# Sums of a Strassen key and value product: formed on VectorE in place of GpSimd

## The chip, the core and the metric

The kernel runs on one core of a Trainium2 chip. The metric is the device time of one execution in microseconds (us), lower is better. Before the change three runs gave 1868.92, 1868.02 and 1868.57 us, a median of 1868.57.

## What is computed

The reference is a decoder trunk of two layers on a stream `x` of 512 tokens by 2048 channels, in float32. The first layer is sparse attention, the second stick-breaking attention. Between them one set of keys and values is computed from the stream, and the change lies in this product:

```python
def shared_kv(x, w_kv):
    b, s, _ = x.shape
    k, v = jnp.split(x @ w_kv, [KVW_B], axis=-1)      # 512x2048 @ 2048x1024
    return k.reshape(b, s, N_KV_B, HEAD_DIM), v.reshape(b, s, N_KV_B, HEAD_DIM)

def mixer_b(x, w_in, w_o, k, v):
    q, gate = jnp.split(x @ w_in, [WIDTH_B], axis=-1)
    ...
```

The queries of `mixer_b`, `x @ w_in[:, :2048]`, are computed right around it: their first 512 columns before, the other three chunks of 512 columns after.

## The kernel before, in words

**Matmuls in parts.** Every float32 operand is split into a high and a low part (`split`, line 140): ScalarE copies the source to the high part, VectorE subtracts that from the source to give the low part. `mm3` (line 144) then makes three matmuls, at lines 145, 146 and 147. Weights stream in from HBM by DMAs from SyncE's queue (`next_raw`, line 191), one 128x2x512 tile for each. The parts of weights are in tiles `wh`/`wl` and `sh`/`sl` of three buffers each, so that ScalarE can write the next part only when TensorE has read an old one.

**The key and value product** is one Strassen step (Winograd's form) of seven half-size products m1 to m7 in place of eight. The stream is cut into halves of tokens and of channels, the weights into halves of rows and into the key and the value columns. `kv_items` (line 423) makes the weight operands in the order in which TensorE takes them: first plain blocks for m2 and m4, then blocks and one difference for m1 and m7, and last, for each of eight k, the three sums of `sums` (line 454). It takes two tiles of weights, r0 and r1. s1 is formed by GpSimd (line 458), s2 and s4 by VectorE (lines 459 and 460); s2 reads s1, and s4 reads s2. Each of the three is then split and used in six matmuls, 18 for each k, for m6, m5 and m3 (`gemm_quarters`, line 471). `sums` for the next k is called ahead of the third split of this one. Every second tile of these weights has its home in the `f` tiles, which is why DMAs and operations of this pass name `f`.

**The last additions.** Keys are gathered in c11 and c12, values in c21 and c22 (they lie in the tiles `E`), each 128x1024. ScalarE copies products out of PSUM into them; VectorE adds m1 to c11, m6 to u (which holds m1), and m5 to c22, in pieces of 128x512. GpSimd makes five 128x1024 additions between tiles of SBUF: c21 + c22 (line 1314) when m7 is out, and behind the last product c21 + u, c22 + u, c12 + t3 and c12 + u (lines 1332 to 1335; t3 holds m3).

**The next Strassen chunks.** The three other query chunks follow at once. In each, a unit is one raw tile: VectorE forms two sums from the raw tile (`prepare`, lines 396 and 397, tile `st`), then s2 and s4 (lines 404 and 405), and these and the plain blocks are split into two items of weights. An item is seven terms of three matmuls with 256 columns, 21 in all: the first two terms use `wh`/`wl`, the next four `sh`/`sl`, the last `wh`/`wl` again. A chunk has 8 units, so 16 items. The two items of unit 0 are made while the key and value pass still has a few matmuls to go (line 1320). The first two sums of unit 1 are not prepared ahead (`u % 8 != 1`, line 417): they come behind the m6 and m5 additions in VectorE's line.

**Order.** Instructions of each engine run in the order of its queue. TensorE's order is written out by hand. On the other engines a scheduler may move instructions, but what runs while `pinned` is set, as through `paced` (line 355), keeps its place. `bg` is a queue of pieces of work: `pumped_at` (line 368) wraps a run of matmul steps (one step is one `mm3`) and issues one piece at each of the listed steps; for the Strassen chunks these are steps 13, 20, 27, 34, 41, 53 and seven later ones of 112 (line 1346). `drain` issues what is left at a chunk's end. In the first chunk `bg` is empty. The keys are read next in the second chunk (`turn_keys`, line 1337) and the values in the third (`split_values`).

Of the kernel before, what the change touches and what calls it, by code (L numbers as in the profile page):

```python
# [14 lines left out]
ALU = mybir.AluOpType  # L15
# [62 lines left out]
def trunk_kernel(  # L78
# [48 lines left out]
    act, dve, pool = (Paced(e) for e in (nc.scalar, nc.vector, nc.gpsimd))  # L127
    pool = nc.gpsimd
# [11 lines left out]
    def split(hi, lo, src, eng=dve):  # L140
        act.activation(hi, src, AF.Copy)
        eng.tensor_tensor(lo, src, hi.bitcast(F32), ALU.subtract)
# [48 lines left out]
    def next_raw():  # L191
        while sent[0] < len(units) and len(raws) < (6 if sent[0] in kv_units else 3):
            raw = homes.get(sent[0])
            if raw is None:
                raw = top.tile([128, 2, 512], F32, name="raw", tag="raw", bufs=3)
            unit = units[sent[0]]
            if len(unit) == 1:
                _, k, n = unit[0].shape
            else:
                k, n = 2, unit[-1]  # L200
            raw = raw.rearrange("p a n -> p (a n)")[:, : k * n].rearrange("p (k n) -> p k n", k=k)
            if len(unit) == 1:
                nc.sync.dma_start(raw, unit[0])
            else:
                src, a, b, c0, n = unit
                rows = src.rearrange("(k p) n -> p k n", p=128)
                step = b - a
                if sent[0] < 2:

                    for i, cut in enumerate(((0, H if sent[0] else NSEL, T), (0, T))):  # L210
                        for lo, hi in zip(cut, cut[1:]):
                            halves.append((raw[:, i, lo:hi], rows[:, a + i * step, c0 + lo : c0 + hi]))
                    if len(halves) == 6:
                        for n in (1, 3, 4, 2, 5, 0):
                            nc.sync.dma_start(*halves[n])
                else:
                    nc.sync.dma_start(raw, rows[:, a : b + 1 : step, c0 : c0 + n])
            raws.append(raw)
            sent[0] += 1
        return raws.popleft()  # L220
# [38 lines left out]
    def weight_parts():  # L259
        return tuple(top.tile([128, 512], F32R, name=n, tag=n, bufs=3) for n in ("wh", "wl"))  # L260
# [92 lines left out]
    bg = deque()  # L353

    def paced(fn, *args):
        was, pinned[0] = pinned[0], True
        fn(*args)
        pinned[0] = was
# [64 lines left out]
    def kv_items(wp):  # L423

        made = [0]
        temps = [F[1][:, n] for n in range(4)]
        for _ in range(2):
            st = wp.tile([128, 4 * H], F32, name="st", tag="st", bufs=2)
            temps.extend(st[:, n * T : (n + 1) * T] for n in range(2))

        def temp():
            made[0] += 1
            return temps[made[0] % 8]

        def parts(n, src):
            if n % 2:
                pair = weight_parts()
            else:
                pair = [wp.tile([128, 4, 128], F32R, name=n, tag=n, bufs=3).rearrange("p a n -> p (a n)") for n in ("sh", "sl")]
            split(*pair, src)  # L440
            return pair

        for k in range(8):
            raw = next_raw()
            for a in range(2):
                yield parts(a, raw[:, a])
        for k in range(8):
            raw = next_raw()
            s3 = temp()
            dve.tensor_tensor(s3, raw[:, 0], raw[:, 1], ALU.subtract)  # L450
            yield parts(0, raw[:, 0])
            yield parts(1, s3)

        def sums():
            r0 = next_raw()
            r1 = next_raw()
            s1, s2, s4 = temp(), temp(), temp()
            pool.tensor_tensor(s1, r0[:, 1], r1[:, 1], ALU.add)
            dve.tensor_tensor(s2, s1, r0[:, 0], ALU.subtract)
            dve.tensor_tensor(s4, r1[:, 0], s2, ALU.subtract)  # L460
            return s2, s1, s4

        ready = sums()
        for k in range(8):
            three = ready
            for n, src in enumerate(three):
                if n == 2 and k < 7:
                    ready = sums()
                yield parts(3 * k + n, src)
# [809 lines left out]
    with tc.tile_pool(name="sp", bufs=1) as sp:  # L1279
        Kf, Vf = shared  # L1280
        banks = [bank(b, "q") for b in range(4)]
        gemm = gemm_w(kitems, plain, banks, order=PAIRS)
        items = first_chunk(gemm, TF, T1, C3, lambda: Ahead(kv_items(sp), 4))
        for h in range(4):
            act.activation(F[0][:, h], banks[h], AF.Copy)


        def pair(first, name):
            return [bank(first + j, name) for j in range(2)]

        def half(row, t):
            return lambda k: (XH[k + row][:, t : t + H], XL[k + row][:, t : t + H])

        def summed(i):
            return lambda k: (C3[k][0][:, i], C3[k][1][:, i])

        c11, c12, c21, c22 = Kf[:, 0:2], Kf[:, 2:4], Vf[:, 0:2], Vf[:, 2:4]
        u, t3 = F[3][:, 2:4], F[1][:, 0:2]

        m2, m4 = pair(4, "m2"), pair(6, "m4")  # L1300
        run(gemm_quarters(items, ((half(8, 0), m2), (summed(2), m4))))
        for j in range(2):
            paced(act.activation, c11[:, j], m2[j], AF.Copy)
        for j in range(2):
            paced(lambda: act.activation(c21[:, j], m4[j], AF.Copy, scale=-1.0))

        m1, m7 = pair(0, "m1"), pair(2, "m7")
        run(gemm_quarters(items, ((half(0, 0), m1), (summed(1), m7))))
        for j in range(2):
            paced(act.activation, u[:, j], m1[j], AF.Copy)  # L1310
            paced(dve.tensor_tensor, c11[:, j], c11[:, j], m1[j], ALU.add)
        for j in range(2):
            paced(act.activation, c22[:, j], m7[j], AF.Copy)
        pool.tensor_tensor(c21, c21, c22, ALU.add)

        m6, m5, m3 = pair(4, "m6"), pair(6, "m5"), pair(0, "m3")
        gemm = gemm_quarters(items, ((summed(0), m6), (half(0, H), m5), (half(8, H), m3)))
        steps(gemm, 42)
        pinned[0] = True
        items = strassen_stream([512] * 3, sp).prime()  # L1320
        pinned[0] = False
        steps(gemm, 2)
        for j in range(2):
            paced(dve.tensor_tensor, u[:, j], u[:, j], m6[j], ALU.add)
        steps(gemm, 2)
        for j in range(2):
            paced(act.activation, c12[:, j], m5[j], AF.Copy)
            paced(dve.tensor_tensor, c22[:, j], c22[:, j], m5[j], ALU.add)
        run(gemm)
        for j in range(2):  # L1330
            paced(act.activation, t3[:, j], m3[j], AF.Copy)
        pool.tensor_tensor(c21, c21, u, ALU.add)
        pool.tensor_tensor(c22, c22, u, ALU.add)
        pool.tensor_tensor(c12, c12, t3, ALU.add)
        pool.tensor_tensor(c12, c12, u, ALU.add)

        def turn_keys(g):
            s = slice(g * 128, (g + 1) * 128)
            ps = bank(0, "kt")
            for t in range(4):  # L1340
                pe.transpose(ps[:, t * 128 : (t + 1) * 128], Kf[:, t, s], ident)
            act.activation(Kf[:, :, s], ps.rearrange("p (t s) -> p t s", t=4), AF.Copy)

        for n, dst in enumerate(F[1:]):
            M = product_banks(2 - n)
            gemm = pumped_at(gemm_s(items, C3, M), (13, 20, 27, 34, 41, 53, 65, 77, 89, 101, 104, 107, 110))
            if n == 1:
                steps(gemm, 40)
                for g in range(4):
                    steps(gemm, 16)  # L1350
                    turn_keys(g)
            run(gemm)
            drain()
            if n == 2:
                items = Ahead(gate_items(), 2).prime()
                combined = combine_last(sp, M, lambda i: quarter(dst, i))
            else:
                bg.extend(combine(sp, M, lambda i: quarter(dst, i)))
            if n == 1:

                bg.extend(lambda t=t: split_values(t) for t in range(4))
                bg.append(lambda: split_keys(0))
                bg.extend(lambda i=i: split_scaled(0, i) for i in (3, 1, 2))
# [298 lines left out]
```

## Time and profile before

| what | value |
|---|---|
| median of three runs | 1868.57 us (1868.02 to 1868.92) |
| the profiled execution, its time | 1868.31 us |
| its span, first to last instruction | 1866.6 us |
| mean granted TensorE clock | 0.998 |
| ScalarE busy | 940.0 us, 50% of the span |
| mean DMA rate | 106 GB/s |
| GpSimd, eight 128x512 additions at line 458 | 6.3 + 5.9 us |
| GpSimd, five 128x1024 additions | 2.4 to 2.8 us each |

How to read the rows below. PE is TensorE's matmuls, PEld its weight loads, DVE VectorE, ACT ScalarE, POOL GpSimd, SP SyncE. A timeline row gives the start in us from the span's beginning, the duration, the engine, the source line, the operation, output and inputs, and in brackets the idle time just before it with what ended it. `x2` on a timeline row is two merged instructions with their time together. A row of waits gives who waited for whom, the total in us, the number of waits, the longest. A row of groups gives busy us and the mean ns of one. A row of windows gives the stretch and its length, the busy time and count of PE, PEld, DVE, ACT and POOL, then the granted TensorE clock, the busy share of DMA and GB/s. Most operations pass through a helper that records them, so their line is L118 or L116; they are told apart by tiles.

### The profile page before, as it was taken

Reading aid. Unit: us, or ns where it says so; the run is one execution under the profiler, and the core shown is the slowest. Engines: PE = TensorE matmul, PEld = TensorE weight load, DVE = VectorE, ACT = ScalarE, POOL = GpSimd, SP = SyncE. Lnnn points to the kernel's source line nnn. Section 1 sums busy time; section 2 is a strip of 40 time slices with the busy share of each in tenths; the row PEclk is TensorE's granted clock in tenths of the full one; section 3 lists DMA queues with packets and bytes.
Section 4 is the critical chain, followed back from the end, with each engine's and each line's share of the span. In section 5 each row is a group of like instructions: output and inputs, shape, how many; then the busy total and the mean of one; then the engine's idle time right before and its main releaser. Section 6 shows DMA issues by size and latency. Waiting matters only on the chain.

```text
span 1866.6 us, 24141 instructions
## 1 busy us (share of the span) xinstructions
PE 1852.5 (99%) x8845; PEld 1561.0 (84%) x8845; DVE 1233.7 (66%) x2337; ACT 940.0 (50%) x1686; POOL 36.7 (2%) x41
## 2 busy tenths in 40 slices
PE   9999999999999999999999989999999999999998
PEld 8898888888888888888888879997888888888887
DVE  5668678566556444675467698888878745567534
ACT  3546333355554432475245534467888743347422
POOL 0000000000000000000000040001000000000000
PEclk9999999999999999999999999999999999999999
DMA  6441323222221432323335633322122252232323
GB/s 198 128 123 59 102 90 102 90 68 68 68 69 57 159 123 79 125 95 109 124 118 164 212 127 103 102 91 91 57 68 80 68 186 96 76 128 99 116 102 113
DMA packets 111431, 197.55 MB, mean 106 GB/s; under 512 B 8784, under 2 KB 29264, under 8 KB 111312
## 3 DMA queue, kind: packets, MB, share of 16 engines
q1 hardware_dynamic: 111312, 196.01, 32.7%
q8 instruction: 69, 1.13, 0.2%
q14 instruction: 50, 0.41, 0.1%
HBM read 187.60 MB, written 8.39 MB: 105 GB/s over the span
## 4 chain that ended last, share of the span: by engine, by line
PE 96%; DVE 2%; issue 1%; ACT 1%; DMA 0%; SPq 0%; DVEq 0%; ACTq 0%
PE g L145 12%; PE g L147 12%; PE g L146 12%; PE o L146 7%; PE o L145 7%; PE o L147 7%; PE q L147 4%; PE q L146 4%; PE q L145 4%; PE m L147 3%; PE m L146 3%; PE m L145 3%; PE iq L147 1%; PE iq L146 1%; PE iq L145 1%; PE pt L949 1%
## 5 line engine op out<-in xcount | busy, mean ns | idle before, releaser
L118 ACT ACTIVATE wh<-raw 128x512 fp32r<-128x512 f32 (+2 forms) x596 | 345.3, 580 | 660.7 <-PE g L146 219.6
L118 DVE TENSOR_TENSOR wl<-raw,wh 128x512 fp32r<-128x512 f32 (+2 forms) x595 | 372.9, 628 | 432.3 <-ACT wh L118 417.3
L145 PE MATMUL g<-xh,wh 128*128 128x512 f32 x1024 | 403.5, 394 | 0.0
L147 PE MATMUL g<-xh,wl 128*128 128x512 f32 x1024 | 399.5, 390 | 0.0
L146 PE MATMUL g<-xl,wh 128*128 128x512 f32 x1024 | 399.3, 390 | 0.0
L147 PEld LDWEIGHTS g<-xh,wl 128*128 128x128 f32 x1024 | 192.2, 188 | 40.9
L146 PEld LDWEIGHTS g<-xl,wh 128*128 128x128 f32 x1024 | 192.5, 188 | 37.4
L145 PEld LDWEIGHTS g<-xh,wh 128*128 128x128 f32 x1024 | 192.4, 188 | 36.9
L147 PE MATMUL o<-xh,wl 128*128 128x512 f32 x512 | 199.2, 389 | 0.0
L146 PE MATMUL o<-xl,wh 128*128 128x512 f32 x512 | 199.2, 389 | 0.0
L145 PE MATMUL o<-xh,wh 128*128 128x512 f32 x512 | 199.2, 389 | 0.0
L145 PE MATMUL q<-xh,wh 128*128 128x512 f32 x320 | 124.5, 389 | 0.0
L146 PE MATMUL q<-xl,wh 128*128 128x512 f32 x320 | 124.5, 389 | 0.0
L147 PE MATMUL q<-xh,wl 128*128 128x512 f32 x320 | 124.5, 389 | 0.0
L145 PEld LDWEIGHTS o<-xh,wh 128*128 128x128 f32 x512 | 96.1, 188 | 20.0
L147 PEld LDWEIGHTS o<-xh,wl 128*128 128x128 f32 x512 | 96.1, 188 | 20.0
L146 PEld LDWEIGHTS o<-xl,wh 128*128 128x128 f32 x512 | 96.1, 188 | 19.9
L146 PEld LDWEIGHTS q<-xl,wh 128*128 128x128 f32 x320 | 60.1, 188 | 12.6
L145 PEld LDWEIGHTS q<-xh,wh 128*128 128x128 f32 x320 | 60.1, 188 | 12.6
L147 PEld LDWEIGHTS q<-xh,wl 128*128 128x128 f32 x320 | 60.1, 188 | 12.3
L116 ACT ACTIVATE wk<-z 128x512 f32<-128x512 f32 x80 | 47.9, 598 | 38.7 <-DVE z L116 15.2
L118 DVE TENSOR_TENSOR xl<-f,xh 128x512 fp32r<-128x512 f32 x80 | 54.3, 686 | 12.6 <-ACT f L118 12.3
(341 smaller groups left out, 3237.1 us busy)
## 6 DMA issues: line engine op xcount, KB each, us to landing
raw<-w_in_a SPq DMA_DIRECT2D x95, 512.0 KB, 3.6
raw<-w_in_b SPq DMA_DIRECT2D x64, 512.0 KB, 3.7
raw<-w_ple_gate SPq DMA_DIRECT2D x52, 512.0 KB, 3.4
raw<-w_o_a SPq DMA_DIRECT2D x24, 512.0 KB, 3.4
raw<-w_o_b SPq DMA_DIRECT2D x24, 512.0 KB, 3.5
f<-w_kv_b SPq DMA_DIRECT2D x16, 512.0 KB, 4.1
raw<-w_kv_b SPq DMA_DIRECT2D x16, 512.0 KB, 3.8
raw<-w_ple_gate SPq DMA_DIRECT2D x24, 256.0 KB, 2.8
```

The source lines that it names most:

```text
L116: ins = method(*args, **kw)
L118: ins = method(*args, **kw)
L145: pe.matmul(out, a[0], b[0], start=start, stop=False)
L146: pe.matmul(out, a[0], b[1], start=False, stop=False)
L147: pe.matmul(out, a[1], b[0], start=False, stop=stop)
L949: pe.transpose(pt[:, h * 128 : (h + 1) * 128], P[i][:, h, kb * 128 : (kb + 1) * 128], ident)
```

## The change

Three edits. `sums` forms s1 on VectorE. The addition c21 + c22 at line 1314 and the two c22 + m5 additions at line 1328 are taken out. In place of the four GpSimd additions behind the last product, six VectorE additions of 128x1024 are appended to `bg`: c21 + c22 (c22 still holds m7 alone), c22 + c12 (c12 still holds m5), c12 + t3, c12 + u, c21 + u, c22 + u. So one is issued at each of the first six listed steps of the first Strassen chunk.

```diff
@@ -455,7 +455,7 @@
             r0 = next_raw()
             r1 = next_raw()
             s1, s2, s4 = temp(), temp(), temp()
-            pool.tensor_tensor(s1, r0[:, 1], r1[:, 1], ALU.add)
+            dve.tensor_tensor(s1, r0[:, 1], r1[:, 1], ALU.add)
             dve.tensor_tensor(s2, s1, r0[:, 0], ALU.subtract)
             dve.tensor_tensor(s4, r1[:, 0], s2, ALU.subtract)
             return s2, s1, s4
@@ -1311,7 +1311,6 @@
             paced(dve.tensor_tensor, c11[:, j], c11[:, j], m1[j], ALU.add)
         for j in range(2):
             paced(act.activation, c22[:, j], m7[j], AF.Copy)
-        pool.tensor_tensor(c21, c21, c22, ALU.add)
 
         m6, m5, m3 = pair(4, "m6"), pair(6, "m5"), pair(0, "m3")
         gemm = gemm_quarters(items, ((summed(0), m6), (half(0, H), m5), (half(8, H), m3)))
@@ -1325,14 +1324,11 @@
         steps(gemm, 2)
         for j in range(2):
             paced(act.activation, c12[:, j], m5[j], AF.Copy)
-            paced(dve.tensor_tensor, c22[:, j], c22[:, j], m5[j], ALU.add)
         run(gemm)
         for j in range(2):
             paced(act.activation, t3[:, j], m3[j], AF.Copy)
-        pool.tensor_tensor(c21, c21, u, ALU.add)
-        pool.tensor_tensor(c22, c22, u, ALU.add)
-        pool.tensor_tensor(c12, c12, t3, ALU.add)
-        pool.tensor_tensor(c12, c12, u, ALU.add)
+        for out, more in ((c21, c22), (c22, c12), (c12, t3), (c12, u), (c21, u), (c22, u)):
+            bg.append(lambda out=out, more=more: dve.tensor_tensor(out, out, more, ALU.add))
 
         def turn_keys(g):
             s = slice(g * 128, (g + 1) * 128)
```

## The prediction

> **What bounds the kernel now.** I began with the page, parts 1 and 4, and then asked for TensorE's own waits.
>
> ```profile
> PE 1852.5 (99%) x8845; PEld 1561.0 (84%) x8845; DVE 1233.7 (66%) x2337; ACT 940.0 (50%) x1686; POOL 36.7 (2%) x41
> PE 96%; DVE 2%; issue 1%; ACT 1%; DMA 0%; SPq 0%; DVEq 0%; ACTq 0%
> ```
>
> ```profile
> PE m L147 <- DVE wl L118: 5.9, 1, 5.9
> PE m L146 <- DVE wl L118: 1.1, 1, 1.1
> PE z L145 <- DVE t L116: 0.2, 1, 0.2
> ```
>
> TensorE is busy 99% of the span. VectorE or GpSimd can shorten the run only where TensorE stands still or runs slowly. From these waits, two such places matter, both for a low part `wl` from VectorE. The timeline of TensorE dates them (start, duration, instruction), and the windows give the granted clock (the third column from the right).
>
> ```profile
> 1078.87 0.39 PE L145 MATMUL m<-sh,xh 128*128 128x512 f32 x1
> 1080.23 0.39 PE L145 MATMUL m<-wh,xh 128*128 128x512 f32 x1
> 1081.72 0.50 PE L146 MATMUL m<-wl,xh 128*128 128x512 f32 x1 [1.10 <-DVE wl L118]
> ...
> 1107.62 0.28 PE L145 MATMUL m<-xh,wh 128*128 128x256 f32 x1
> 1112.83 0.28 PE L146 MATMUL m<-xl,wh 128*128 128x256 f32 x1
> 1118.98 0.58 PE L147 MATMUL m<-xh,wl 128*128 128x256 f32 x1 [5.88 <-DVE wl L118]
> 1124.84 0.28 PE L147 MATMUL m<-c,sl 128*128 128x256 f32 x1
> 1126.39 0.28 PE L145 MATMUL m<-xh,wh 128*128 128x256 f32 x1
> 1156.63 0.28 PE L145 MATMUL m<-xh,wh 128*128 128x256 f32 x1
> ```
>
> ```profile
> 1081.00:1083.00 2.00, 1.28 (x6) 1.06 (x7) 2.00 (x4) 0.00 (x0) 0.12 (x1) 1.00 0.68 258
> 1119.00:1121.00 2.00, 2.00 (x9) 2.00 (x10) 1.84 (x4) 1.47 (x4) 0.00 (x0) 0.50 0.00 0
> ```
>
> Place one is in the last key and value pass. Six matmuls take 1080.23 - 1078.87 = 1.36 us there, 0.227 each; the step from 1080.23 to 1081.72 is 1.49, so 1.26 are lost.
>
> Place two is the first Strassen chunk, which runs from 1107.62 (X below) to 1156.63, where the next begins: 49.01 us. It is 16 items of 21 matmuls. Twelve undisturbed items take 1156.63 - 1126.39 = 30.24, so 2.52 an item and 0.12 a matmul; 16 items would take 40.32. Lost: 8.69. Of this the wait is 6.03 (from 1112.83 + 0.12 to 1118.98). Another 2.6 is a clock of 0.50 after it: the 27 matmuls from 1118.98 to 1124.84 take 5.86 where 27 x 0.12 = 3.24 is normal.
>
> [...]
>
> Why was `wl` late? VectorE and GpSimd side by side:
>
> ```profile
> 1109.24 4.26 DVE L118 TENSOR_TENSOR st<-raw 128x256 f32<-128x256 f32 x2
> 1113.42 2.56 DVE L118 TENSOR_TENSOR st<-st,raw 128x256 f32<-128x256 f32 x1
> 1116.01 2.44 DVE L118 TENSOR_TENSOR st<-raw,st 128x256 f32<-128x256 f32 x1
> 1118.38 0.55 DVE L118 TENSOR_TENSOR wl<-raw,wh 128x384 fp32r<-128x384 f32 x1
> ...
> 1110.64 2.58 POOL L1334 TENSOR_TENSOR E<-E,f 128x1024 f32<-128x1024 f32 x1
> 1115.66 2.52 POOL L1335 TENSOR_TENSOR E<-E,f 128x1024 f32<-128x1024 f32 x1
> ...
> 1075.39 1.78 DVE L118 TENSOR_TENSOR f<-st,raw 128x512 f32<-128x512 f32 x1
> 1077.20 2.77 DVE L118 TENSOR_TENSOR f<-f,f 128x512 f32<-128x512 f32 x1
> 1079.90 1.76 DVE L118 TENSOR_TENSOR wl<-st,wh 128x512 fp32r<-128x512 f32 x1
> ...
> 1076.58 2.85 POOL L1314 TENSOR_TENSOR E<-E 128x1024 f32<-128x1024 f32 x1
> ```
>
> A VectorE addition that meets a GpSimd addition grows to the latter's length: 2.44 beside 2.52, 2.77 beside 2.85. The next groups show what these shapes take alone (mean ns last before the idle time).
>
> ```profile
> L118 DVE TENSOR_TENSOR st<-raw 128x256 f32<-128x256 f32 x14 | 5.3, 419 | 0.0
> L118 DVE TENSOR_TENSOR sl<-st,sh 128x512 fp32r<-128x512 f32 x15 | 10.4, 692 | 1.7 <-ACT sh L118 1.7
> L118 DVE TENSOR_TENSOR c<-E,c 128x768 fp32r<-128x768 f32 x8 | 7.6, 955 | 0.4 <-ACT c L118 0.3
> ```
>
> So the four GpSimd additions at the end do not run beside VectorE. They hold up the four instructions that make the sums for items 2 and 3.
>
> **The change, part by part.** VectorE's rows first: s2 and s4 of one k, s2 of the next, and the two c22 additions.
>
> ```profile
> 1095.50 0.68 DVE L118 TENSOR_TENSOR st<-f,raw 128x512 f32<-128x512 f32 x1
> 1096.22 0.69 DVE L118 TENSOR_TENSOR st<-f,st 128x512 f32<-128x512 f32 x1
> ...
> 1098.63 0.68 DVE L118 TENSOR_TENSOR st<-st,raw 128x512 f32<-128x512 f32 x1
> ...
> 1108.05 1.28 DVE L118 TENSOR_TENSOR E<-E,m 128x512 f32<-128x512 f32 x2
> ```
>
> *The eight s1 additions and the c21 addition leave GpSimd.* Place one: its three VectorE instructions were held. Without that, VectorE starts at 1075.39 with s1, then s2 and s4 (0.72 each to the next, since each needs the one before), then `wl`: 1075.39 + 3 x 0.72 + 0.69 = 1078.24. TensorE asks at 1080.23 + 0.23. Early by 2.2, so 1.26 come back. If that failed, none would. For the rest of the pass: from s2 of one k to s2 of the next (1095.50 to 1098.63) is 3.13 us where no GpSimd work meets it. With s1 on VectorE, 3.13 + 0.72 = 3.85, against 18 matmuls x 0.227 = 4.08 on TensorE. It fits, with 0.23 to spare; cost nothing. If that cover went, a k would cost what VectorE takes over 4.08.
>
> *The four last GpSimd additions go, and so do the two c22 + m5 additions in VectorE's line (the last row).* The first sums of item 2 then start at 1108.05 instead of 1109.24, at X + 0.43, and run at full speed. Place two's 8.69 come back, clock included, unless the new additions cost some.
>
> *Six 128x1024 additions enter VectorE's line.* In the built order they stand: none in unit 1 (items 2, 3), two each in units 2 and 3, one each in units 4 and 5. The trace has no such form on VectorE. From 419, 692 and 955 the steps are 0.27, so 1.22 long. Since two 128x256 instructions follow each other in 0.67 while each lasts 0.42, one takes about 0.08 less of the line than its length: a = 1.14. Bounds: four of the steps alone (1.07) and two 128x512 additions one behind the other (0.60 each, from 1.28 for the two less 0.68: 1.20). The 768 row is nearest; I take 1.14. [...]
>
> A unit without additions, from the second chunk (first sum, s2, s4, `sl`, next unit's first sum):
>
> ```profile
> 1157.93 0.75 DVE L118 TENSOR_TENSOR st<-raw 128x256 f32<-128x256 f32 x2
> 1158.60 0.42 DVE L118 TENSOR_TENSOR st<-st,raw 128x256 f32<-128x256 f32 x1
> 1159.06 0.43 DVE L118 TENSOR_TENSOR st<-raw,st 128x256 f32<-128x256 f32 x1
> 1160.24 0.69 DVE L118 TENSOR_TENSOR sl<-st,sh 128x512 fp32r<-128x512 f32 x1 [0.29 <-ACT sh L118]
> 1161.92 0.76 DVE L118 TENSOR_TENSOR st<-raw 128x256 f32<-128x256 f32 x2
> ```
>
> That is 3.99 us from 1157.93 to the unit's end at 1161.92, against 5.04 for two items on TensorE. Units start at X + 0.43, 4.42, then 4.42 + 3.99 + 2.28 = 10.69, 16.96, 22.09, 27.22. The first `sl` of a unit with one addition ahead of it is ready 0.67 + 1.14 + 0.46 + 1.18 + 0.69 = 4.14 after its start. Unit 3: X + 14.83; TensorE reads it 0.96 into item 6 (the ninth matmul), at 15.12 + 0.96 = 16.08: early. Unit 4: 21.10 against 20.16 + 0.96 = 21.12: just even, and the weight load comes 0.12 ahead of its matmul, so some 0.15 late. Unit 5: 26.23 against 26.16, another 0.1. Unit 6, without addition, is early again. New waits: 0.3; with a = 1.07 none, with 1.20 about 0.6. Waits this short leave the clock alone, as the 1.1 us one did.
>
> *Queues.* ACT's, SP's and TensorE's orders are the same in both builds; no DMA moves. GpSimd's queue gets shorter. Nothing after 1156.63 holds TensorE but one wait of 0.2, so a shift there reaches the end.
>
> **Sum.** -1.26 - 8.69 + 0.3 = -9.65. The profiled execution took 1868.31 (span 1866.6 and 1.7 around it): 1858.66. The median of the runs, 1868.57, is 0.26 above it: **1858.9**.
>
> **Rivals.**
> *A, the additions overrun.* 6 x 1.14 = 6.84 against a slack of 4 x 1.05 = 4.2 in units 2 to 5: 2.64 short, covered by the lead with which the chunk starts. If that lead is gone (unit 1 starts some 2.4 later), TensorE pays 2.64: 1868.57 - 9.95 + 2.64 = 1861.3. Against it: unit 1 starts where the dropped c22 additions stood.
> *B, place one stays.* Only 8.69 - 0.3: 1860.2. Against it: 2.2 us in hand.
> *C, something later takes it back*, half of it: 1863.7. Nothing in the waits points there.
> *D, the change does not do what it says:* VectorE's long instructions have another cause, and stay: 1868.6. Against it: lengths pair up row by row.
> *E, slower: the transfer wait moves into VectorE's line.* On GpSimd the s1 additions waited for their rows:
>
> ```profile
> POOL st L458 <- DMA f<-w_kv_b: 9.9, 3, 4.3
> 1070.18 1.30 POOL L458 TENSOR_TENSOR st<-raw,f 128x512 f32<-128x512 f32 x1 [4.27 <-DMA f<-w_kv_b]
> ```
>
> VectorE's queue is in order, so splits behind such a wait would wait too. At 3.3 us each (9.9 / 3), eight cost 26.4, less 8 x 0.23 slack, 24.6 net: 1868.57 + 24.6 - 9.65 = 1883.5. It decides against the change from (9.65 + 1.8) / 8 = 1.4 us each. Against it: the third s1 found its row at 1070.18, and VectorE's turn for it is 1075.39, 5.2 later.
>
> **How the numbers follow.** Forecast 0.62; A 0.20, B 0.06, C 0.05, D 0.03, E 0.04. The range runs from all 9.95 back, less the runs' own half microsecond (1858.0, widened to 1857.6 for the bounds of a), to 1861.5, which takes in A and B: 0.88. What a measurement of this kernel can tell from no change is about 0.2%, 3.7 us. Faster by more: forecast, A, B and C, 0.93; within: D, 0.03; slower: E, 0.04.
>
> **What would show it.** In the changed kernel's profile TensorE's two waits for `wl` are gone; the granted clock stays 1.00 after 1110; the chunk takes 40.3 to 41; VectorE's sums last 0.42 and 0.69 throughout; the additions last 1.22; small waits for `sl`, if any, sit 20 to 27 us into the chunk. I am wrong if VectorE waits for transfers at s1, if additions last over 1.3, or if a wait of over 3 us appears and the clock drops with it.

## The result, and the profile after

| | before | after |
|---|---|---|
| median | 1868.34 us, four runs (1868.02 to 1868.92) | 1858.58 us, four runs (1858.43 to 1858.86) |
| span of the profiled execution | 1866.6 us | 1857.0 us |
| last key and value pass, 144 matmuls | 34.19 us | 32.64 us |
| first Strassen chunk, 336 matmuls | 49.01 us | 40.44 us |

The change makes the kernel 9.8 us faster. The ratio of the times is 0.9948, with an interval from 0.993 to 0.9965. The forecast was 1858.9, with a range from 1857.6 to 1861.5.

The profile is read in the same order as before. First the page's busy time and chain of the changed kernel, then TensorE's waits.

```profile
PE 1850.0 (100%) x8845; PEld 1559.3 (84%) x8845; DVE 1226.7 (66%) x2349; ACT 939.7 (51%) x1686; POOL 11.8 (1%) x28
PE 97%; DVE 2%; ACT 1%; issue 0%
```

```profile
PE spun L167 <- DVE xl L118: 1.4, 1, 1.4
PE z L145 <- DVE t L116: 0.2, 1, 0.2
```

Both waits for `wl` are gone; the 1.4 us at the very start was there before too. GpSimd keeps 11.8 of its 36.7 busy us. VectorE's busy time went down, from 1233.7 to 1226.7 us, although it has twelve instructions more: the time in which it is held counts as busy, and s2 of unit 1, which lasted 2.56 us before, lasts 0.42 here.

TensorE's timeline of the changed kernel gives the two places: the first matmul of the last pass, the first one of the chunk (X is now 1106.56), two small gaps, and the first of the next chunk. Below it stands the start of the last pass in the kernel before.

```profile
1073.92 0.39 PE L145 MATMUL m<-sh,c 128*128 128x512 f32 x1
...
1106.56 0.28 PE L145 MATMUL m<-xh,wh 128*128 128x256 f32 x1
...
1127.67 0.33 PE L147 MATMUL m<-c,sl 128*128 128x256 f32 x1
1127.84 0.28 PE L145 MATMUL m<-c,sh 128*128 128x256 f32 x1
...
1132.75 0.37 PE L147 MATMUL m<-c,sl 128*128 128x256 f32 x1
1132.96 0.28 PE L145 MATMUL m<-c,sh 128*128 128x256 f32 x1
...
1147.00 0.28 PE L145 MATMUL m<-xh,wh 128*128 128x256 f32 x1
```

```profile
1073.43 0.39 PE L145 MATMUL m<-sh,c 128*128 128x512 f32 x1
```

The pass takes 1106.56 - 1073.92 = 32.64 us, which is 144 steps of 0.2267: nothing is lost. Before, it took 1107.62 - 1073.43 = 34.19, so 1.55 came back. The chunk takes 1147.00 - 1106.56 = 40.44 against 40.32 without any gap: 8.57 came back. Both together are 10.12, but the span fell by 9.6 only. The difference is the 0.49 us by which the last pass starts later here. It is no cost of the change: the ten other kernels below have this start at 1073.7 to 1074.1, among them tail_alone, which is the kernel before up to that point, at 1073.80. So the profiled execution of before was early here.

The windows of the changed kernel show the granted clock (third column from the right) at 1.00 where it had been 0.50:

```profile
1117.00:1119.00 2.00, 2.00 (x19) 2.00 (x18) 2.00 (x5) 0.29 (x1) 0.00 (x0) 1.00 0.52 130
1119.00:1121.00 2.00, 2.00 (x19) 2.00 (x18) 1.68 (x5) 1.05 (x3) 0.00 (x0) 1.00 0.38 140
```

And these are the first sums of each of VectorE's units in the chunk, with the group of the new additions:

```profile
1106.99 0.75 DVE L118 TENSOR_TENSOR st<-raw 128x256 f32<-128x256 f32 x2
...
1110.91 0.76 DVE L118 TENSOR_TENSOR st<-raw 128x256 f32<-128x256 f32 x2
1111.59 1.22 DVE L118 TENSOR_TENSOR E<-E 128x1024 f32<-128x1024 f32 x1
1112.72 0.42 DVE L118 TENSOR_TENSOR st<-st,raw 128x256 f32<-128x256 f32 x1
...
1117.17 0.75 DVE L118 TENSOR_TENSOR st<-raw 128x256 f32<-128x256 f32 x2
...
1123.43 0.75 DVE L118 TENSOR_TENSOR st<-raw 128x256 f32<-128x256 f32 x2
...
1128.55 0.75 DVE L118 TENSOR_TENSOR st<-raw 128x256 f32<-128x256 f32 x2
```

```profile
L118 DVE TENSOR_TENSOR E<-E,f 128x1024 f32<-128x1024 f32 x4 | 4.9, 1219 | 0.0
```

Against X the units start at 0.43, 4.35, 10.61, 16.87 and 21.99, where the prediction had 0.43, 4.42, 10.69, 16.96 and 22.09. An addition lasts 1.22 and takes 1112.72 - 1111.59 = 1.13 of the line.

### The profile page after: what moved, and what is told of

It is laid out like the page before. It is cut to its first block, busy times and chain, and to the rows that moved or that the text cites. A ratio compares the mean times of both kernels' runs of the same rounds, so it can differ in the third digit from the quotient of the medians.

```text
span 1857.0 us, 24116 instructions
## 1 busy us (share of the span) xinstructions
PE 1850.0 (100%) x8845; PEld 1559.3 (84%) x8845; DVE 1226.7 (66%) x2349; ACT 939.7 (51%) x1686; POOL 11.8 (1%) x28
## 3 DMA queue, kind: packets, MB, share of 16 engines
q8 instruction: 69, 1.13, 0.2%
## 4 chain that ended last, share of the span: by engine, by line
PE 97%; DVE 2%; ACT 1%; issue 0%
PE g L145 12%; PE g L147 12%; PE g L146 12%; PE o L146 7%; PE o L147 7%; PE o L145 7%; PE q L147 4%; PE q L146 4%; PE q L145 4%; PE m L147 4%; PE m L145 4%; PE m L146 4%; PE iq L147 1%; PE iq L145 1%; PE iq L146 1%; PE pt L949 1%
```

## The experiments

The theory under test: a GpSimd addition that reads SBUF holds a VectorE addition that meets it until it is through, so the four last ones hold up item 2 of the chunk, and the wait that follows halves TensorE's clock. The rivals: the long VectorE instructions have another cause; only the bunching at one point without lead mattered; the moved s1 additions were the main cost.

All kernels in one table; the kernel before, run beside them, had medians from 1868.13 to 1868.44. The pass and the chunk are measured as above, from the first matmul to the next stage's first.

| kernel | median us | last pass | chunk | TensorE's waits for `wl`/`sl` in the chunk |
|---|---|---|---|---|
| before | 1868.34 | 34.19 | 49.01 | 5.9 |
| after | 1858.58 | 32.64 | 40.44 | none listed |
| s1_alone | 1867.15 | 32.64 | 48.99 | 6.1 |
| tail_alone | 1859.05 | 32.64 | 40.44 | none listed |
| tail_later | 1858.49 | 32.64 | 40.31 | none listed |
| tail_at_once | 1865.08 | 32.64 | 47.10 | 4.4 |
| tail_spread_gpsimd | 1865.2 | 32.64 | 46.83 | 1.4, 0.6, 2.0 |
| gpsimd_reads | 1866.99 | 32.63 | 48.71 | 5.7 |
| gpsimd_writes | 1858.72 | 32.65 | 40.46 | none listed |
| tail_doubled | 1866.37 | 32.64 | 47.98 | 2.1, 1.7, 0.8 |
| four_at_once | 1862.46 | 32.64 | 43.07 | 2.1 |
| five_at_once | 1863.83 | 32.64 | 45.31 | 3.3 |

### Which part brings the time: s1_alone and tail_alone

s1_alone is the kernel before with the first line of the diff alone; tail_alone is the changed kernel with that line taken back:

```diff
-            dve.tensor_tensor(s1, r0[:, 1], r1[:, 1], ALU.add)
+            pool.tensor_tensor(s1, r0[:, 1], r1[:, 1], ALU.add)
```

> The kernel before, with only the eight s1 additions moved to VectorE; all five 128x1024 additions stay on GpSimd. My theory: place two (8.6 us, the four last additions holding up the sums of items 2 and 3) is untouched, place one mostly returns: about 1867.0 us, the 5.9 us wait for wl and the slow clock behind it still there. Rival, the s1 additions were the larger cost: near 1860.

> The changed kernel with the eight s1 additions put back on GpSimd; the 128x1024 additions stay on VectorE. My theory: place two returns whole. Without c21 + c22 in the way, place one returns too: two held instructions of 1.1 us more put the first wl of the last pass at about 1079.7, still ahead of TensorE at 1080.5, and 4.24 us a k against 4.08 uses up 1.3 us of lead over eight k. About 1858.9, no wait in the last key and value pass. Rival, moving s1 is needed for place one: 1860.1, with the wait near 1081 still there.

s1_alone came to 1867.15 us, ratio 0.9994 (0.9985 to 1.0003), so it can't be told from the kernel before by its time alone; its trace shows the pass without loss and the chunk with all of it. TensorE's wait, and the GpSimd additions beside which it arises, in s1_alone:

```profile
PE m L147 <- DVE wl L118: 6.1, 1, 6.1
```

```profile
1107.36 2.40 POOL L1334 TENSOR_TENSOR E<-E,f 128x1024 f32<-128x1024 f32 x1 [30.16 <-ACT f L118]
1109.72 2.57 POOL L1332 TENSOR_TENSOR E<-E,f 128x1024 f32<-128x1024 f32 x1
```

tail_alone came to 1859.05 (0.995, 0.9936 to 0.9965) and has the pass without loss as well. VectorE's rows of tail_alone around place one:

```profile
1075.15 1.66 DVE L118 TENSOR_TENSOR sl<-st,sh 128x512 fp32r<-128x512 f32 x1 [0.35 <-ACT sh L118]
1076.73 0.68 DVE L118 TENSOR_TENSOR f<-st,raw 128x512 f32<-128x512 f32 x1
...
1078.05 0.68 DVE L118 TENSOR_TENSOR wl<-st,wh 128x512 fp32r<-128x512 f32 x1
```

One GpSimd s1 holds one VectorE instruction for 1 us (1.66 instead of 0.69), and `wl` is still ready at 1078.73. So place one needed the s1 additions *and* the c21 addition on GpSimd; taking away either clears it. Once the others are gone, moving the s1 additions brings nothing in these two places: TensorE's pass and chunk are the same to 0.01 us. The 0.47 us between the medians of tail_alone and the changed kernel must come from elsewhere. TensorE's last matmul starts at 1851.52 there and at 1851.75 in the changed kernel, so in the profiled executions the difference lies behind it; its cause stays open.

### Is it GpSimd, and is it its reads: gpsimd_reads and gpsimd_writes

Both are the changed kernel with useless GpSimd work behind VectorE's m6 additions, on a tile that is free at the time. VectorE's fill of one column starts it.

```diff
+        dummy = F[2][:, 0:2]
+        paced(dve.memset, dummy[:, 0, 0:1], 0.0)
+        for _ in range(4):                     # gpsimd_writes: range(8)
+            tc.keep_in_program_order(pool.tensor_tensor(dummy, dummy, u, ALU.add))
+                                               # gpsimd_writes: pool.memset(dummy, 0.0)
```

> The changed kernel with four extra GpSimd additions of 128x1024 on a tile that nobody needs at the time, started behind VectorE's m6 additions. My theory: VectorE's sums of unit 1 are held for about 10 us again, TensorE waits some 6 us for wl and its clock halves: 1867 to 1870. Rival, the long VectorE instructions had to do with the tiles or data and not with GpSimd: 1858.6.

> The changed kernel with eight extra GpSimd fills (memset) of 128x1024 of that tile at the same place, which write and do not read. If only GpSimd's reads stand in the way of VectorE's two-input additions: 1858.6 and sums of 0.42 us throughout. If any GpSimd work does: like the reads, 1866 to 1870.

gpsimd_reads: 1866.99 us. GpSimd's and VectorE's rows:

```profile
1107.42 9.95 POOL L1327 TENSOR_TENSOR f<-f,f 128x1024 f32<-128x1024 f32 x4 [919.10 <-DVE f L118]
```

```profile
1107.52 2.63 DVE L118 TENSOR_TENSOR st<-raw 128x256 f32<-128x256 f32 x1
1110.07 2.61 DVE L118 TENSOR_TENSOR st<-st,raw 128x256 f32<-128x256 f32 x1
1112.72 2.44 DVE L118 TENSOR_TENSOR st<-raw,st 128x256 f32<-128x256 f32 x1
1115.08 2.70 DVE L118 TENSOR_TENSOR wl<-raw,wh 128x384 fp32r<-128x384 f32 x1
```

Each of four GpSimd additions stretches one VectorE instruction, on tiles that have nothing to do with the sums. gpsimd_writes: 1858.72 us. The same rows there:

```profile
1107.00 8.05 POOL L1327 MEMSET f<- 128x1024 f32 x8 [918.86 <-DVE f L118]
```

```profile
1107.13 0.42 DVE L118 TENSOR_TENSOR st<-raw 128x256 f32<-128x256 f32 x1
1107.46 0.42 DVE L118 TENSOR_TENSOR st<-st,raw 128x256 f32<-128x256 f32 x1
1107.92 0.42 DVE L118 TENSOR_TENSOR st<-raw,st 128x256 f32<-128x256 f32 x1
```

GpSimd is busy for 8 us and VectorE does not notice. The rival of another cause is out. The eight fills write twice as many tiles as the four additions and read none, so what is left for the conflict is that the additions read SBUF; that an addition is also another operation than a fill was not tested apart. The same three sums last 2.44 to 2.63 us beside the additions and 0.42 beside the fills.

### Engine or place: tail_spread_gpsimd, tail_at_once, tail_later

The first keeps the changed kernel's places and returns the engine; the second keeps the engine and gives up the places; the third spreads the additions more widely.

```diff
 tail_spread_gpsimd
-            bg.append(lambda ...: dve.tensor_tensor(out, out, more, ALU.add))
+            bg.append(lambda ...: on_gpsimd(out, more))   # one-column dve copy of out onto itself, then
+                                                          # pool.tensor_tensor(out, out, more, ALU.add)
 tail_at_once
-            bg.append(lambda ...: dve.tensor_tensor(out, out, more, ALU.add))
+            paced(dve.tensor_tensor, out, out, more, ALU.add)
 tail_later
-(13, 20, 27, 34, 41, 53, ...)
+(13, 27, 41, 55, 69, 83) if n == 0 else (13, 20, 27, 34, 41, 53, ...)
```

> The changed kernel, but the six spread 128x1024 additions run on GpSimd; at each of the six steps VectorE makes a one-element copy that the GpSimd addition waits for, so they are as far apart as in the changed kernel. My theory, that a GpSimd addition holds VectorE for its whole length wherever it stands: each costs VectorE some 2.4 us instead of 1.13, units 2 to 5 fall about 8 us behind TensorE: 1866 to 1868, more if single waits halve the clock. Rival, it was only that four stood together at the one point without lead: about 1858.6.

tail_spread_gpsimd came to 1865.2 us. Two GpSimd additions and the VectorE instructions that met them:

```profile
1112.00 2.44 POOL L1332 TENSOR_TENSOR E<-E 128x1024 f32<-128x1024 f32 x1 [923.49 <-DVE E L118]
1116.38 2.58 POOL L1332 TENSOR_TENSOR E<-E,E 128x1024 f32<-128x1024 f32 x1 [1.94 <-ACT sh L118]
```

```profile
1112.21 2.51 DVE L118 TENSOR_TENSOR st<-raw,st 128x256 f32<-128x256 f32 x1
...
1116.62 2.89 DVE L118 TENSOR_TENSOR sl<-st,sh 128x512 fp32r<-128x512 f32 x1
```

Spreading does not save it: an addition on GpSimd takes 2.51 - 0.42 = 2.1 or 2.89 - 0.69 = 2.2 us out of VectorE's line, and on VectorE itself 1.13. I had put 2.4 for each, and 8 us in all; the chunk lost 46.83 - 40.31 = 6.5, so the time lies under the 1866 to 1868 expected. The smaller price accounts for some 6 x 0.25 = 1.5 of that; since the 6.5 hold the slow clock behind the last wait as well, the 8 were too many by more than the price explains.

> The changed kernel, but the six 128x1024 additions run in one go ahead of unit 1's sums instead of at six steps of the chunk. My theory: wl of item 2 is ready at X + 0.43 + 6 x 1.13 + 2.02 = X + 9.2 where TensorE wants it at X + 5.3, so a wait of 3.9 us: 1862.5 if the clock stays at 1.00, 1865 if so long a wait halves it. Rival, only GpSimd as a neighbour costs anything and the placing does not matter: 1858.6.

tail_at_once came to 1865.08 us (0.9982, 0.9972 to 0.9991), with this wait and this clock:

```profile
PE m L147 <- DVE wl L118: 4.4, 1, 4.4
```

```profile
1116.00:1118.00 2.00, 1.70 (x8) 1.70 (x9) 1.77 (x4) 1.78 (x4) 0.00 (x0) 0.50 0.00 0
```

The engine alone is a third of the gain: without the spreading 6.5 of the 9.8 us are lost again. Engine and place are both needed.

> The changed kernel with the six additions one to a unit, at steps 13, 27, 41, 55, 69 and 83 of the first chunk. Each unit then takes 5.1 us on VectorE against 5.04, and the lead of the start covers it: the two small gaps of the changed kernel (0.05 and 0.09 us) vanish. About 1858.5, no difference that can be measured. Rival: additions inside later units collide with the second chunk's start and lose some tenths.

tail_later came to 1858.49; the chunk takes 40.31 us and the two small gaps are gone. It is 0.13 us less in the chunk, which the times can't tell from the changed kernel.

### How much room is left on VectorE: tail_doubled

```diff
+        def there_and_back(out, more):
+            dve.tensor_tensor(out, out, more, ALU.add)
+            dve.tensor_tensor(out, out, more, ALU.add)
```

> The changed kernel with each of the six additions done twice, so the keys and values hold some terms twice. Twelve additions of 1.13 us: 13.6 against 4.2 of slack in units 2 to 5 and the lead. By my units the first sl of unit 5 is ready at X + 32.9 where TensorE wants it at X + 26.2: 6.7 us lost in waits of 1 to 3 us each: 1865.3 with the clock at 1.00 throughout. Rival, the clock drops with them: 1868 or more. If VectorE had more slack than I read: under 1862.

It came to 1866.37 us, a little over the 1865.3 expected. Two of its three waits, and the clock behind each:

```profile
1123.95 0.38 PE L147 MATMUL m<-xh,wl 128*128 128x256 f32 x1 [2.09 <-DVE wl L118]
...
1132.73 0.39 PE L147 MATMUL m<-xh,wl 128*128 128x256 f32 x1 [1.72 <-DVE wl L118]
```

```profile
1126.00:1128.00 2.00, 2.00 (x12) 2.00 (x11) 1.97 (x4) 0.00 (x0) 0.00 (x0) 0.50 0.00 0
...
1134.00:1136.00 2.00, 2.00 (x19) 2.00 (x18) 2.00 (x5) 0.28 (x1) 0.00 (x0) 1.00 0.40 75
```

The reckoning by units holds (waits in units 3, 4 and 5, where the changed kernel has two small gaps), but I was wrong on the clock: it was halved behind the wait of 2.09 us.

### How long a wait halves the clock: four_at_once, five_at_once

```diff
+            if n < 4:                          # five_at_once: 5
+                paced(dve.tensor_tensor, out, out, more, ALU.add)
+            else:
+                bg.append(lambda ...: dve.tensor_tensor(out, out, more, ALU.add))
```

> The changed kernel with four of the six additions ahead of unit 1's sums and two spread. With all six there TensorE waited 4.4 us; each addition took about 1.2 of VectorE's line, so the wait here should be 4.4 - 2 x 1.2 = 2.0. If a wait of 2 us halves the clock, as one wait of 2.09 us did with the additions doubled, some 2.6 us come on top: 1863.2. If it doesn't: 1860.6 and a granted clock of 1.00. [...]

> The same with five additions ahead and one spread: a wait of 4.4 - 1.2 = 3.2 us. With the clock halved behind it 1864.4, with the clock at 1.00 1861.8. If the wait has to pass some length between 2 and 3.2 us to halve the clock, this one halves it and the one with four does not.

four_at_once, its wait and the window behind it in the profiled execution:

```profile
PE m L147 <- DVE wl L118: 2.1, 1, 2.1
```

```profile
1114.00:1116.00 2.00, 1.97 (x14) 1.82 (x15) 1.79 (x4) 1.52 (x4) 0.00 (x0) 1.00 0.00 0
```

and five_at_once:

```profile
PE m L147 <- DVE wl L118: 3.3, 1, 3.3
```

```profile
1116.00:1118.00 2.00, 2.00 (x12) 2.00 (x11) 2.00 (x6) 0.95 (x3) 0.00 (x0) 0.50 0.06 12
```

The wait of 2.1 us left the clock alone in this profiled execution, which took 1861.25 us, near the 1860.6 expected without it. Its five runs took 1861.25 to 1862.99, though, and the changed kernel's four lie within 0.43 us; the median is 1862.46. The mean granted clock was 1.000 in the profiled run and 0.998 to 0.999 in the other four, where tail_alone, which has no such wait, has 0.999 to 1.000. That points to a clock halved at the wait in some of those four; it is not shown, since only the profiled run left a trace. With the wait of 3.3 us the clock was halved: 1863.83.

## Why the prediction was right

- **Place one** was named rightly and sized too small: 1.26 us in the prediction, 1.55 measured. I took the one long step and left out what came behind it: the kernel before has further long steps (0.33 to 1082.05, 0.26 to 1085.96, 0.33 to 1086.29 where 0.227 is normal). That either edit alone returns it was not part of the prediction.
- **Place two** carried the change: 8.69 lost before, of which 8.57 came back. The step that the four last additions hold up the four instructions which make the sums for items 2 and 3 is shown by gpsimd_reads, which puts the loss back with additions that do nothing else.
- **The cost of the new additions** was forecast as 0.3 us of waits for `sl` in units 4 and 5. It came to 0.05 and 0.09, at 1127.84 and 1132.96, behind the first `sl` of items 8 and 10, as named. The prediction's own rows give 0.19 rather than 0.3: unit 5 is late by 26.23 + 0.12 - 26.16 = 0.19 in all, and the 0.10 of unit 4 is part of that and not ahead of it. The unit's own cost was a few hundredths smaller than the rows of the second chunk had it, so the units ran up to 0.1 us ahead of the sum.
- **The price of an addition**, 1.22 long and 1.14 of the line, extrapolated from three shapes, was measured as 1.22 and 1.13.
- **Sum.** -9.65 forecast, -9.76 between the medians. In the two traces the places gave 0.29 and 0.18 more than forecast, and the early last pass in the profiled execution of before took 0.49 off the difference of the spans. That the forecast came so close is partly luck: two terms were each too small by a few tenths, and in the spans the early start of one profiled execution made up for them. What made up for them between the medians is not shown.
- **Rivals.** A, the overrun, did not come, since the lead held; tail_doubled shows where it does. B and D are out by the traces, D by gpsimd_reads. C did not come: from the end of the chunk to TensorE's last matmul it is 1861.33 - 1156.63 = 704.70 us before and 1851.75 - 1147.00 = 704.75 after. E did not come: VectorE listed no wait for a transfer in this stretch.

## What to carry to other kernels

An engine that is off the critical path can still slow the one that is on it: GpSimd, busy for 2% of the span before, held VectorE's sums (2.56 us in place of 0.42), and through them TensorE waited 5.88 us. Look for instructions of one form that last 0.4 us in one place and 2.5 in another, and lay the neighbour's rows beside them: work "moved out of the way" to GpSimd took about twice as much out of VectorE's line here (2.1 to 2.2 us for each 128x1024 addition) as it takes on VectorE itself (1.13). Then place the moved work where each unit has room for it, and reckon the lead unit by unit; with the same additions in one go, two thirds of the gain were lost again.

## What the runs showed of the hardware

In two traces the clock fell at different lengths of time after a wait began. These windows of one microsecond, from the kernel before and from tail_doubled, show when:

```profile
1117.00:1118.00 1.00, 0.00 (x0) 0.00 (x0) 1.00 (x1) 0.00 (x0) 1.00 (x1) 0.95 0.00 0
...
1124.00:1125.00 1.00, 1.00 (x8) 1.00 (x7) 1.00 (x3) 0.33 (x1) 0.00 (x0) 0.63 0.00 0
...
1865.00:1866.00 1.00, 0.00 (x0) 0.00 (x0) 0.00 (x0) 0.00 (x0) 0.00 (x0) 0.71 0.12 38
```

```profile
1125.00:1126.00 1.00, 1.00 (x5) 1.00 (x6) 1.00 (x1) 0.50 (x2) 0.00 (x0) 0.54 0.00 0
...
1128.00:1129.00 1.00, 1.00 (x8) 1.00 (x8) 1.00 (x4) 0.00 (x0) 0.00 (x0) 0.76 0.17 33
...
1862.00:1863.00 1.00, 0.00 (x0) 0.00 (x0) 0.00 (x0) 0.00 (x0) 0.00 (x0) 0.68 0.43 143
```

A clock of 0.95 over one microsecond is 0.90 us at 1.00, which the windows ahead of it have, and 0.10 at 0.50, which those behind it have. So in the kernel before the clock fell at 1117.90, 4.80 us into the wait (1118.98 - 5.88 = 1113.10), and was back at 1124.74, 6.84 us later. In tail_doubled it fell at 1125.08, 3.22 us after the wait of 2.09 us began (1123.95 - 2.09 = 1121.86) and 1.1 us after it was over, and was back at 1128.48, 3.40 later. Behind the last matmul it falls again, at 1865.42 and 1862.36: 747.52 and 737.28 us after the first fall. These two distances differ by 10.24, three times 3.4133, and the slow stretches are about two and one times that long. My estimate from these numbers is that the clock changes at points 3.4133 us apart: 747.52 is 219 such steps and 737.28 is 216. The windows of three other runs have half clock for 3.4 us (tail_spread_gpsimd, five_at_once) or 6.8 (tail_at_once), about one step or two; in s1_alone and gpsimd_reads the matmuls behind the wait come 0.21 us apart for 5.3 and 5.7 us, where 0.12 is normal. So the slow 5.86 us in the prediction are the part of those 6.84 in which TensorE had work.

By this estimate the waits differ in how much of them lies between two such points. The waits of 1.99 us (tail_spread_gpsimd, 1130.00 to 1131.99, clock down at 1132.12) and 2.09 us (tail_doubled, 1121.86 to 1123.95) lie between two of them, and the clock was halved. The wait of 1.72 us in tail_doubled, from 1131.01 to 1132.73, is cut by the point at 1125.08 + 2 x 3.4133 = 1131.91. In four_at_once the only fall is the one behind the last matmul:

```profile
1857.00:1858.00 1.00, 0.00 (x0) 0.00 (x0) 0.00 (x0) 0.00 (x0) 0.00 (x0) 0.87 0.62 209
```

It is at 1857.74, and 218 of the estimated steps earlier is 1113.63: the wait from 1111.91 to 1114.03 is cut into 1.72 and 0.40. Both these waits left the clock at 1.00. So, by the estimate, idle time of up to 1.72 us between two points left the clock alone in these traces, and 1.99 us halved it. If the place of the points relative to a wait differs from run to run, that would explain the spread of the times of four_at_once; with one trace of it, that is not shown.
